# Two weight sums and three low halves of a quad by accumulating loads on GpSimd's queue

## The chip, the cores and the metric

One core of a Trainium2 chip runs the whole program. The metric is the device time of one execution in microseconds (us). Profiles and traces are of one execution each; their times are counted from the start of its span.

## The reference, cut to what matters

One layer of an encoder trunk, for 512 tokens of width 1024 in float32: a gated feed-forward block, a mixer (attention in a neighbourhood beside a pooled branch), a second feed-forward block, and a gated embedding, each normalized before and after and added to the residual. The change lies in the two feed-forward blocks:

```python
D_MODEL = 1024
SEQ = 512
D_FF = 2816

def swiglu(x, w_gate, w_up, w_down):
    return (jax.nn.silu(x @ w_gate) * (x @ w_up)) @ w_down

f = swiglu(rms_norm(h, ffn1_pre_g[i]), ffn1_w_gate[i], ffn1_w_up[i], ffn1_w_down[i])
h = h + 0.5 * rms_norm(f, ffn1_post_g[i])
```

## The kernel before

TensorE multiplies in a rounded float32 form, so every operand is split into a high half `hi` (the value rounded) and a low half `lo` (the value minus `hi`), and a product is three matmuls, at L277 to L279: `hi` with `hi`, `hi` with the other's `lo`, `lo` with the other's `hi`. The weights come as a stream of 195 chunks of 128x1024 float32 (512 KB) from `in_wst`. The class `Stream` loads a chunk on SyncE's queue into a tile `raw` (L207; five buffers), lets ScalarE cast it to `hi` (L243) and VectorE subtract `hi` from it to make `lo` (L244, shown by its helper's line, L165). `hi` and `lo` lie in a tile `w`, of which there are six, so a chunk is split when the product six before it has been multiplied.

The hidden width of a feed-forward block is worked in 11 groups, in three parts of 3, 4 and 4 groups (`PARTS`); each part ends with a down projection over its groups. Groups 3 to 10 (`FAST`), four in each of the last two parts and 16 in the two blocks together, are quads: four weight blocks, a21, a22, a11 and a12, enter seven products of half the width instead of eight (`fast_group`). The operands on the weights' side are

- product 0: a11; 1: a12; 2: a11 + a21 + a22; 3: a21 + a11; 4: a21 + a22; 5: a22; 6: a12 + a11 + a21 + a22.

Products 0, 2, 4 and 6 are summed in PSUM bank `p`, product 1 in `q`, products 3 and 5 in `r`. ScalarE copies `p` to `m1` after product 0, `p` to `acc` after product 2 and `r` to `m7` after product 3 (L477); VectorE adds and subtracts the others. A bank can't be written by the next product before it has been read.

The weight sums are made in `source`: when product 2 is prepared, VectorE makes `both` = a21 + a22 in a buffer of its own (`wsum`), then a21 + a11 in a21's tile and a11 + `both` in a11's tile; for product 6 it adds that to a12. `pump` splits the next chunks in time, at most `NB` = 6 ahead of what has been multiplied; `load` starts loads in the order of the stream, and a chunk's load waits until a tile `raw` is free. The order on each engine is set by the order in which the code is recorded and by a scheduler, which lets an instruction pass others of its engine that it does not depend on. GpSimd has only constants to set at the start.

Of the kernel before, what the change touches and what calls it, by code (L numbers as in the profile page):

```python
# [10 lines left out]
F32 = mybir.dt.float32  # L11
F32R = mybir.dt.float32r
AF = mybir.ActivationFunctionType
ALU = mybir.AluOpType

P = 128
# [7 lines left out]
CH = 1024  # L24
# [2 lines left out]
PARTS = ((0, 3), (3, 7), (7, 11))  # L27
FAST = range(3, 11)
NB = 6
NRAW = 5  # L30
RAW_AHEAD = 2
SPLIT_AHEAD = 4

# [85 lines left out]
def kernel(  # L119
# [9 lines left out]
    nc = tc.nc  # L129
    n_chunks = wst.shape[0]  # L130

    const = ctx.enter_context(tc.tile_pool(name="const", bufs=1))
    wraw = ctx.enter_context(tc.tile_pool(name="wraw", bufs=NRAW))
    wsum = ctx.enter_context(tc.tile_pool(name="wsum", bufs=1))
    wsp = ctx.enter_context(tc.tile_pool(name="wsp", bufs=NB))
    act = ctx.enter_context(tc.tile_pool(name="act", bufs=1))
    tmp = ctx.enter_context(tc.tile_pool(name="tmp", bufs=2))
# [23 lines left out]
    def f32(ap):  # L161
        return ap.bitcast(F32)

    def tt(o, a, b, op):
        nc.vector.tensor_tensor(o, a, b, op=op)  # L165
# [5 lines left out]
    class Stream:  # L171

        LOADS = (3, 4, 4, 4, 4, 4, 4)

        def __init__(self):
            self.ops = []
            self.needs = []
            self.shift = []  # L180
            chunk = 0
            for kind in plan():
                quad = kind == 2
                for i in range(7 if quad else 1):
                    self.ops.append((quad, chunk, i))
                    self.needs.append(chunk + (self.LOADS[i] if quad else 1))
                    self.shift.append(24 if quad and i in (2, 5) else 16 if kind else 0)
                chunk += 4 if quad else 1
            self.n = len(self.ops)
            assert chunk == n_chunks  # L190
            self.loaded = 0
            self.split = 0
            self.done = 0
            self.hold = False
            self.freed = set()
            self.over = set()
            self.raw = {}
            self.parts = {}
            self.both = None

        def load(self, upto):
            while self.loaded < min(upto, n_chunks) and (self.loaded < NRAW or self.loaded - NRAW in self.over):
                c = self.loaded
                self.raw[c] = wraw.tile([P, CH], F32, tag="raw", name=f"raw{c}")
                w = CH // 4 if c < 1 else CH
                for i in range(0, CH, w):
                    nc.sync.dma_start(self.raw[c][:, i:i + w], wst[c][:, i:i + w])  # L207
                self.loaded += 1

        def drop(self, *chunks):  # L210
            for c in chunks:
                del self.raw[c]
                self.over.add(c)

        def source(self, n):

            kind, c, i = self.ops[n]
            if not kind:
                return self.raw[c], (c,)
            a21, a22, a11, a12 = (self.raw.get(c + j) for j in range(4))  # L220
            if i == 2:
                self.both = wsum.tile([P, CH], F32, tag="sum", name="both")
                tt(self.both, a21, a22, ALU.add)
                tt(a21, a21, a11, ALU.add)
                tt(a11, a11, self.both, ALU.add)
            if i == 6:
                tt(a12, a12, a11, ALU.add)
            return ((a11, ()), (a12, ()), (a11, ()), (a21, (c,)), (self.both, ()), (a22, (c + 1,)),
                    (a12, (c + 2, c + 3)))[i]

        def pump(self, upto):
            while self.split < min(upto, self.done + NB, self.n):
                c = self.split
                self.load(self.needs[c])
                assert self.loaded >= self.needs[c]
                raw, over = self.source(c)
                both = wsp.tile([P, 2 * CH + 128], F32R, tag="w", name=f"w{c}")
                b = self.shift[c]
                hi, lo = both[:, b:b + CH], both[:, b + CH + 64:b + 2 * CH + 64]
                w = CH // 4 if c < 1 else CH  # L240
                for i in range(0, CH, w):
                    sl = slice(i, i + w)
                    nc.scalar.copy(hi[:, sl], raw[:, sl])  # L243
                    tt(lo[:, sl], raw[:, sl], f32(hi[:, sl]), ALU.subtract)  # L244
                self.drop(*over)
                self.parts[c] = (hi, lo)
                self.split += 1
                self.load(self.needs[c] + RAW_AHEAD)
# [801 lines left out]
def plan():  # L1050

    def ffn(first):
        out = []
        for g0, g1 in PARTS:
            for g in range(g0, g1):
                out += [2] if g in FAST else [first if g == 0 else 0] * 4
            out += [0] * (g1 - g0) + [int(g1 == PARTS[-1][1])] * (g1 - g0)
        return out

    mixer = [1] * 4 + [0] * (3 * 4 + 1 + 16 + 8 + 4) + [1] * 4  # L1060
    return ffn(0) + mixer + ffn(1) + [0] * 3 + [1] * 8
# [114 lines left out]
```

## Time and profile before

| What | us |
|---|---|
| median of 3 runs | 1083.73 (1081.83 to 1085.82) |
| the profiled execution | 1084.12 |
| its span | 1082.3 |
| TensorE busy | 1060.2 (98%) |
| VectorE busy | 762.3 (70%) |
| ScalarE busy | 544.2 (50%) |
| GpSimd busy | 0.7 |
| SyncE's queue: 107.01 MB | 31.7% of the 16 DMA engines' span |

The profile names engines PE (matmuls), PEld (weight loads), DVE (VectorE), ACT (ScalarE), POOL (GpSimd) and SP (SyncE). A matmul's length is modelled and overlaps the next one's; what counts is the distance of their starts, and the waits. "Idle before" is the time that an engine stood still ahead of a group, with what ended it. The DMA share is the busy share of the 16 DMA engines, which can come out a little over 1 where packets overlap.

### The profile page before, as it was taken

The numbers are of one execution on the slowest core, as the hardware profiler recorded it, in microseconds if no ns is written. First come the engines' busy times: TensorE is split into PE (matmuls) and PEld (weight loads), VectorE is DVE, ScalarE is ACT, GpSimd is POOL, SyncE is SP. The second block draws the span as 40 slices with busy tenths as digits, with TensorE's granted clock in tenths as the row PEclk, the third lists the DMA queues.
The fourth block names the chain that finished last, engine by engine and source line by source line (L and its number), as shares of the span: only waits on it lengthen the run. The fifth ranks groups of instructions, "written<-read, shape, count | busy, mean of one in ns | idle before, by whom it ended". The sixth has DMA issues, their size and how long they took to land.

```text
span 1082.3 us, 16827 instructions
## 1 busy us (share of the span) xinstructions
PE 1060.2 (98%) x6762; PEld 955.9 (88%) x6762; DVE 762.3 (70%) x1279; ACT 544.2 (50%) x921; POOL 0.7 (0%) x6
## 2 busy tenths in 40 slices
PE   9999999999999999999999999999999999999994
PEld 7788999889999988877888899888999889999894
DVE  7893787558854987977444429994787558854976
ACT  8552555235543765366222247752555235543874
POOL 0000000000000000000000000000000000000000
PEclk9999999999999999999999999999999999999997
DMA  8331335223362342231333321342235223341202
GB/s 297 107 104 59 87 109 157 78 78 104 111 178 50 108 153 79 78 98 45 99 96 95 97 76 40 107 133 72 81 115 155 79 79 100 109 162 60 63 17 79
DMA packets 37023, 108.12 MB, mean 100 GB/s; under 512 B 4816, under 2 KB 11472, under 8 KB 36944
## 3 DMA queue, kind: packets, MB, share of 16 engines
q1 hardware_dynamic: 36800, 107.01, 31.7%
q8 instruction: 53, 0.87, 0.3%
q14 instruction: 26, 0.21, 0.1%
q10 hardware_dynamic: 144, 0.03, 0.0%
HBM read 104.93 MB, written 2.10 MB: 99 GB/s over the span
## 4 chain that ended last, share of the span: by engine, by line
PE 90%; DVE 6%; ACT 3%; issue 0%; DMA 0%; DVEq 0%; ACTq 0%
PE g L277 14%; PE g L278 14%; PE g L279 14%; PE p L278 6%; PE p L279 6%; PE p L277 6%; PE r L278 3%; PE r L279 3%; PE r L277 3%; PE gate L279 2%; PE gate L277 2%; PE gate L278 2%; PE q L278 1%; PE q L279 1%; PE q L277 1%; PE br L277 1%
## 5 line engine op out<-in xcount | busy, mean ns | idle before, releaser
L165 DVE TENSOR_TENSOR w<-raw,w 128x1024 fp32r<-128x1024 f32 (+1 forms) x227 | 273.7, 1208 | 152.6 <-ACT w L243 152.4
L243 ACT CAST w<-raw 128x1024 fp32r<-128x1024 f32 (+1 forms) x227 | 234.7, 1038 | 262.1 <-PE g L279 131.5
L277 PE MATMUL g<-zh,w 128*128 128x512 f32 (+1 forms) x512 | 178.6, 349 | 0.0
L278 PE MATMUL g<-zl,w 128*128 128x512 f32 (+1 forms) x512 | 178.3, 348 | 0.0
L279 PE MATMUL g<-zh,w 128*128 128x512 f32 (+1 forms) x512 | 178.3, 348 | 0.0
L279 PE MATMUL g<-uh,w 128*128 128x256 f32 (+1 forms) x448 | 146.5, 330 | 1.4 <-DVE w L165 1.4
L278 PE MATMUL g<-ul,w 128*128 128x256 f32 (+1 forms) x448 | 147.4, 330 | 0.2 <-DVE ul L168 0.2
L277 PE MATMUL g<-uh,w 128*128 128x256 f32 (+1 forms) x448 | 146.4, 331 | 0.6 <-ACT w L243 0.6
L278 PEld LDWEIGHTS g<-zl,w 128*128 128x128 f32 x512 | 96.6, 189 | 12.4
L279 PEld LDWEIGHTS g<-zh,w 128*128 128x128 f32 x512 | 96.2, 188 | 12.6
L277 PEld LDWEIGHTS g<-zh,w 128*128 128x128 f32 x512 | 96.2, 188 | 12.4
L279 PEld LDWEIGHTS g<-uh,w 128*128 128x128 f32 x448 | 84.7, 190 | 9.7 <-DVE w L165 1.6
L278 PEld LDWEIGHTS g<-ul,w 128*128 128x128 f32 x448 | 85.4, 191 | 8.5 <-DVE ul L168 0.6
L277 PEld LDWEIGHTS g<-uh,w 128*128 128x128 f32 x448 | 84.8, 190 | 8.8 <-ACT w L243 0.9
L279 PE MATMUL p<-uh,w 128*128 128x256 f32 x256 | 71.9, 281 | 0.0
L278 PE MATMUL p<-ul,w 128*128 128x256 f32 x256 | 71.9, 281 | 0.0
L277 PE MATMUL p<-uh,w 128*128 128x256 f32 x256 | 71.9, 281 | 0.0
L278 PE MATMUL p<-x,w 128*128 128x256 f32 x256 | 71.5, 279 | 0.0
L278 PE MATMUL r<-x,w 128*128 128x256 f32 x256 | 71.5, 279 | 0.0
L279 PE MATMUL p<-x,w 128*128 128x256 f32 x256 | 71.5, 279 | 0.0
L279 PE MATMUL r<-x,w 128*128 128x256 f32 x256 | 71.4, 279 | 0.0
L277 PE MATMUL p<-x,w 128*128 128x256 f32 x256 | 71.4, 279 | 0.0
(195 smaller groups left out, 2187.6 us busy)
## 6 DMA issues: line engine op xcount, KB each, us to landing
raw<-in_wst SPq DMA_DIRECT2D x191, 512.0 KB, 3.6
h<-in_x SPq DMA_DIRECT2D x8, 256.0 KB, 5.5
bm<-in_bias SPq DMA_DIRECT2D x64, 32.0 KB, 2.2
out<-o SPq DMA_DIRECT2D x16, 128.0 KB, 1.7
raw<-in_wst SPq DMA_DIRECT2D x4, 128.0 KB, 4.0
g_sb<-in_gains ACTq DMA_DIRECT2D x1, 34.0 KB, 3.2
edge_sb<-in_edge SPq DMA_DIRECT2D x1, 32.0 KB, 5.3
```

The costliest lines, as they stand in the source:

```text
L165: nc.vector.tensor_tensor(o, a, b, op=op)
L243: nc.scalar.copy(hi[:, sl], raw[:, sl])
L277: nc.tensor.matmul(o, wh, xh, start=first, stop=False, **kw)
L278: nc.tensor.matmul(o, wh, xl, start=False, stop=False, **kw)
L279: nc.tensor.matmul(o, wl, xh, start=False, stop=last, **kw)
```

## The change

Two sums of a quad are no longer made by VectorE. A quad's loads are now five items instead of four chunks: s3 = a21 + a11, s1 = a21 + a22, a22, a11, a12. For s3 and s1 a plain load on SyncE's queue brings the first block, and a second DMA, issued by GpSimd with `accum_op=add`, adds the second block onto it in SBUF. VectorE still makes a11 + s1 and a12 + a11. The low halves of products 0, 1 and 5, whose operand is a single block, are no longer made by VectorE either: ScalarE writes the negated high half into `lo`, and an accumulating DMA of GpSimd adds the block to it, read from `in_wst` once more. The buffer of `both` goes, and there are six `raw` buffers instead of five; all other tiles keep their places.

```diff
-NRAW = 5
+NRAW = 6
...
-    wsum = ctx.enter_context(tc.tile_pool(name="wsum", bufs=1))
...
-        LOADS = (3, 4, 4, 4, 4, 4, 4)
+        ITEMS = ((0, 2), (0, 1), (1,), (2,), (3,))
+        LOADS = (4, 5, 5, 5, 5, 5, 5)
...
+                n = self.loaded
+                c, *more = self.items[n]
+                self.raw[n] = wraw.tile([P, CH], F32, tag="raw", name=f"raw{n}")
                 w = CH // 4 if c < 1 else CH
                 for i in range(0, CH, w):
-                    nc.sync.dma_start(self.raw[c][:, i:i + w], wst[c][:, i:i + w])
+                    nc.sync.dma_start(self.raw[n][:, i:i + w], wst[c][:, i:i + w])
+                for c in more:
+                    nc.gpsimd.dma_start(self.raw[n], wst[c], accum_op=ALU.add)
                 self.loaded += 1
...
+        def single(self, n):
+
+            quad, c, i = self.ops[n]
+            return self.items[c + {0: 3, 1: 4, 5: 2}[i]][0] if quad and i in (0, 1, 5) else None
...
-            a21, a22, a11, a12 = (self.raw.get(c + j) for j in range(4))
+            s3, s1, a22, a11, a12 = (self.raw.get(c + j) for j in range(5))
             if i == 2:
-                self.both = wsum.tile([P, CH], F32, tag="sum", name="both")
-                tt(self.both, a21, a22, ALU.add)
-                tt(a21, a21, a11, ALU.add)
-                tt(a11, a11, self.both, ALU.add)
+                tt(a11, a11, s1, ALU.add)
             if i == 6:
                 tt(a12, a12, a11, ALU.add)
...
                     nc.scalar.copy(hi[:, sl], raw[:, sl])
-                    tt(lo[:, sl], raw[:, sl], f32(hi[:, sl]), ALU.subtract)
+                    if self.single(c) is None:
+                        tt(lo[:, sl], raw[:, sl], f32(hi[:, sl]), ALU.subtract)
+                    else:
+                        nc.scalar.activation(lo, hi, AF.Copy, scale=-1.0)
+                        nc.gpsimd.dma_start(lo, wst[self.single(c)], accum_op=ALU.add)
```

Three places show how the instructions stand. In them `w25` to `w31` are the seven operands of the second quad of the first block (products 0 to 6), `w32` to `w38` those of the third. Of the items after the change, `raw23` to `raw27` are s3, s1, a22, a11 and a12 of the second quad, `raw28` to `raw32` those of the third, and `raw33` and `raw34` are s3 and s1 of the fourth.

On ScalarE, from product 5 of the second quad to product 2 of the third, before (`raw23` is there a22, `raw25` a12 with its sum, `raw28` a11 and `raw29` a12 of the third quad):

```order
L243 CAST w30_1232<-raw23_931 128x1024
L557 CAST zh_1172<-v_1002 128x512
L477 COPY m1_1206<-p_1176 128x512
L243 CAST w31_1265<-raw25_1063 128x1024
L243 CAST w32_1295<-raw28_1293 128x1024
L584 ACTIVATE w_1235<-w_1235 128x256
L477 COPY acc_107<-p_1176 128x512
L243 CAST w33_1328<-raw29_1298 128x1024
L477 COPY m7_1302<-r_1178 128x512
L243 CAST w34_1364<-raw28_1293 128x1024
```

The same place on ScalarE now:

```order
L251 CAST w30_1238<-raw25_1061 128x1024
L569 CAST zh_1178<-v_1005 128x512
L255 ACTIVATE w30_1238<-w30_1238 128x1024
L489 COPY m1_1212<-p_1182 128x512
L251 CAST w31_1272<-raw27_1069 128x1024
L251 CAST w32_1304<-raw31_1302 128x1024
L596 ACTIVATE w_1242<-w_1242 128x256
L255 ACTIVATE w32_1304<-w32_1304 128x1024
L489 COPY acc_104<-p_1182 128x512
L251 CAST w33_1339<-raw32_1308 128x1024
L255 ACTIVATE w33_1339<-w33_1339 128x1024
L489 COPY m7_1313<-r_1184 128x512
```

A negation (L255) stands now ahead of each of the three copies that free a bank.

On VectorE, from the subtraction for product 5 of the second quad to that for product 3 of the third, before:

```order
L165 TENSOR_TENSOR w30_1232<-raw23_931,w30_1232 128x1024
L165 TENSOR_TENSOR zl_1173<-v_1002,zh_1172 128x512
L165 TENSOR_TENSOR raw26_1065<-raw26_1065,raw28_1293 128x1024
L165 TENSOR_TENSOR w31_1265<-raw25_1063,w31_1265 128x1024
L165 TENSOR_TENSOR w_1235<-q_1177,m1_1206 128x512
L165 TENSOR_TENSOR w32_1295<-raw28_1293,w32_1295 128x1024
L165 TENSOR_TENSOR v_1237<-w_1235 128x256
L165 TENSOR_TENSOR raw28_1293<-raw28_1293,both_1360 128x1024
L165 TENSOR_TENSOR w33_1328<-raw29_1298,w33_1328 128x1024
L165 TENSOR_TENSOR raw29_1298<-raw29_1298,raw28_1293 128x1024
L165 TENSOR_TENSOR w34_1364<-raw28_1293,w34_1364 128x1024
L165 TENSOR_TENSOR w_1331<-m7_1302,p_1176 128x512
```

The same place on VectorE now:

```order
L164 TENSOR_TENSOR zl_1179<-v_1005,zh_1178 128x512
L164 TENSOR_TENSOR w31_1272<-raw27_1069,w31_1272 128x1024
L164 TENSOR_TENSOR w_1242<-q_1183,m1_1212 128x512
L164 TENSOR_TENSOR raw31_1302<-raw31_1302,raw29_1172 128x1024
L164 TENSOR_TENSOR v_1244<-w_1242 128x256
L164 TENSOR_TENSOR raw32_1308<-raw32_1308,raw31_1302 128x1024
L164 TENSOR_TENSOR w34_1373<-raw31_1302,w34_1373 128x1024
L164 TENSOR_TENSOR w_1343<-m7_1313,p_1182 128x512
```

The subtractions for `w30`, `w32` and `w33` and the sum of a21 and a11 are gone; the sum with s1 (`raw29`) and the sum for a12 follow each other.

On GpSimd, which had no DMA before, the accumulating loads from product 5 of the first quad to product 5 of the third stand in this order now:

```order
L256 DMA w23_999<-in_wst 128x1024
L256 DMA w25_1065<-in_wst 128x1024
L213 DMA raw28_1071<-in_wst 128x1024
L256 DMA w26_1100<-in_wst 128x1024
L213 DMA raw29_1172<-in_wst 128x1024
L256 DMA w30_1238<-in_wst 128x1024
L256 DMA w32_1304<-in_wst 128x1024
L213 DMA raw33_1310<-in_wst 128x1024
L256 DMA w33_1339<-in_wst 128x1024
L213 DMA raw34_1411<-in_wst 128x1024
L256 DMA w37_1477<-in_wst 128x1024
```

The low half of a quad's product 1 (`w33`) stands behind the first sum of the next quad (`raw33`), whose plain load must land first. `raw31` takes the buffer that `raw24` leaves, and `raw33` that of `raw27`.

## Rows read from the trace of the kernel before

**Rows 1.** The page's first part: busy us, share of the span, instructions.

```profile
PE 1060.2 (98%) x6762; PEld 955.9 (88%) x6762; DVE 762.3 (70%) x1279; ACT 544.2 (50%) x921; POOL 0.7 (0%) x6
```

**Rows 2.** TensorE's waits in the whole span: total us, times, longest us.

```profile
PE nb L343 <- ACT dh L339: 4.1, 2, 2.2
PE nsum L328 <- DVE acc L165: 4.1, 4, 2.5
PE g L279 <- DVE w L165: 1.4, 1, 1.4
...
PE g L278 <- DVE ul L168: 0.2, 1, 0.2
```

**Rows 3.** Timeline of TensorE: start us, us; starts of products in neighbouring quads.

```profile
129.98 0.28 PE L277 MATMUL p<-uh,w 128*128 128x256 f32 x1
...
135.63 0.28 PE L277 MATMUL p<-x,w 128*128 128x256 f32 x1
...
149.60 0.28 PE L277 MATMUL p<-uh,w 128*128 128x256 f32 x1
...
152.43 0.28 PE L277 MATMUL q<-uh,w 128*128 128x256 f32 x1
```

**Rows 4.** Windows: stretch, us, busy by engine, clock, DMA share, GB/s.

```profile
9.00:18.00 9.00, 9.00 (x40) 7.46 (x39) 8.35 (x12) 8.56 (x14) 0.00 (x0) 1.00 1.03 411
15.00:30.00 15.00, 15.00 (x72) 12.52 (x71) 12.73 (x18) 11.08 (x16) 0.00 (x0) 1.00 0.86 298
...
33.70:36.60 2.90, 2.90 (x8) 2.27 (x8) 2.29 (x4) 0.38 (x1) 0.00 (x0) 0.50 0.46 175
...
120.00:140.00 20.00, 20.00 (x173) 20.00 (x173) 17.58 (x21) 11.58 (x17) 0.00 (x0) 1.00 0.36 106
...
192.00:236.00 44.00, 44.00 (x210) 37.03 (x210) 22.40 (x24) 8.97 (x10) 0.00 (x0) 1.00 0.20 60
```

**Rows 5.** VectorE by line and shape: count | busy us, mean ns | idle before.

```profile
L165 DVE TENSOR_TENSOR w<-raw,w 128x1024 fp32r<-128x1024 f32 x223 | 272.1, 1222 | 152.0 <-ACT w L243 151.8
L165 DVE TENSOR_TENSOR raw<-raw,raw 128x1024 f32<-128x1024 f32 x32 | 39.1, 1222 | 4.6 <-DMA raw<-in_wst 4.0
...
L165 DVE TENSOR_TENSOR both<-raw,raw 128x1024 f32<-128x1024 f32 x16 | 19.5, 1221 | 1.8 <-DMA raw<-in_wst 1.6
```

**Rows 6.** Timeline of TensorE where it waited, in brackets, near 30 and 1022 us.

```profile
32.22 0.39 PE L343 MATMUL nb<-dh,ones_r 128*128 128x256 f32 x1 [1.93 <-ACT dh L339]
...
1023.32 0.50 PE L279 MATMUL g<-uh,w 128*128 128x256 f32 x2 [1.45 <-DVE w L165]
```

**Rows 7.** ScalarE by line and shape: count | busy us, mean ns | idle before.

```profile
L243 ACT CAST w<-raw 128x1024 fp32r<-128x1024 f32 x223 | 233.2, 1049 | 261.6 <-PE g L279 131.5 <-PE gate L279 46.5 <-PE br L279 28.9
...
L312 ACT ACTIVATE uh<-h,g_sb 128x256 fp32r<-128x256 f32 x48 | 23.6, 507 | 8.0 <-DVE h L168 7.9
```

**Rows 8.** Timeline of ScalarE in the second quad.

```profile
132.15 0.62 ACT L557 CAST zh<-v 128x512 fp32r<-128x512 f32 x1 [0.23 <-DVE v L165]
133.00 0.59 ACT L477 COPY m<-p 128x512 f32<-128x512 f32 x1 [0.23 <-PE p L279]
...
135.83 1.05 ACT L243 CAST w<-raw 128x1024 fp32r<-128x1024 f32 x1 [1.29 <-PE q L279]
...
139.06 1.05 ACT L243 CAST w<-raw 128x1024 fp32r<-128x1024 f32 x1
```

**Rows 9.** Timeline of VectorE: subtractions for product 6, and for product 4 later.

```profile
134.90 1.22 DVE L165 TENSOR_TENSOR w<-raw,w 128x1024 fp32r<-128x1024 f32 x1
...
148.11 1.23 DVE L165 TENSOR_TENSOR w<-both,w 128x1024 fp32r<-128x1024 f32 x1 [0.44 <-ACT w L243]
```

**Rows 10.** Line 207, SyncE's loads: issue ns and landing us, min/median/max.

```profile
L207 SPq DMA_DIRECT2D raw<-in_wst x195: 327/328/528, 1.2 to 1026.6; - x195
...
DMA to landing us min/median/max: 2.9/3.6/7.5
```

More of the change, by code (lines that the diff above doesn't have):

```diff
@@ L179, in __init__ @@
             self.needs = []
+            self.items = []
             self.shift = []
@@ L184, in __init__ @@
                 for i in range(7 if quad else 1):
-                    self.ops.append((quad, chunk, i))
-                    self.needs.append(chunk + (self.LOADS[i] if quad else 1))
+                    self.ops.append((quad, len(self.items), i))
+                    self.needs.append(len(self.items) + (self.LOADS[i] if quad else 1))
                     self.shift.append(24 if quad and i in (2, 5) else 16 if kind else 0)
+                self.items += [[chunk + j for j in item] for item in (self.ITEMS if quad else ((0,),))]
                 chunk += 4 if quad else 1
@@ L198, in __init__, with drop @@
             self.parts = {}
-            self.both = None
         def load(self, upto):
-            while self.loaded < min(upto, n_chunks) and (self.loaded < NRAW or self.loaded - NRAW in self.over):
-                c = self.loaded
-                self.raw[c] = wraw.tile([P, CH], F32, tag="raw", name=f"raw{c}")
+            while (self.loaded < min(upto, len(self.items))
+                   and (self.loaded < NRAW or self.loaded - NRAW in self.over)):
+                n = self.loaded
+                c, *more = self.items[n]
+                self.raw[n] = wraw.tile([P, CH], F32, tag="raw", name=f"raw{n}")
                 w = CH // 4 if c < 1 else CH
                 for i in range(0, CH, w):
-                    nc.sync.dma_start(self.raw[c][:, i:i + w], wst[c][:, i:i + w])
+                    nc.sync.dma_start(self.raw[n][:, i:i + w], wst[c][:, i:i + w])
+                for c in more:
+                    nc.gpsimd.dma_start(self.raw[n], wst[c], accum_op=ALU.add)
                 self.loaded += 1
[L210 to L213, printed above, removed]
+        def single(self, n):
+            quad, c, i = self.ops[n]
+            return self.items[c + {0: 3, 1: 4, 5: 2}[i]][0] if quad and i in (0, 1, 5) else None
+        def drop(self, *items):
+            for n in items:
+                del self.raw[n]
+                self.over.add(n)
         def source(self, n):
@@ L219, in source @@
                 return self.raw[c], (c,)
-            a21, a22, a11, a12 = (self.raw.get(c + j) for j in range(4))
+            s3, s1, a22, a11, a12 = (self.raw.get(c + j) for j in range(5))
             if i == 2:
-                self.both = wsum.tile([P, CH], F32, tag="sum", name="both")
-                tt(self.both, a21, a22, ALU.add)
-                tt(a21, a21, a11, ALU.add)
-                tt(a11, a11, self.both, ALU.add)
+                tt(a11, a11, s1, ALU.add)
             if i == 6:
                 tt(a12, a12, a11, ALU.add)
-            return ((a11, ()), (a12, ()), (a11, ()), (a21, (c,)), (self.both, ()), (a22, (c + 1,)),
-                    (a12, (c + 2, c + 3)))[i]
+            return ((a11, ()), (a12, ()), (a11, ()), (s3, (c,)), (s1, (c + 1,)), (a22, (c + 2,)),
+                    (a12, (c + 3, c + 4)))[i]
         def pump(self, upto):
```

## Prediction

> **What bounds the kernel now.** I read the busy times first. TensorE is busy for 98% of the span, VectorE for 70%, ScalarE for 50%, GpSimd for nothing [rows 1]. A busy TensorE alone proves little, so the second view is its waits: nine kinds, from 4.1 down to 0.2 us in total, and none of them stands before a matmul that writes `p`, `q` or `r`, which are the banks of the quads [rows 2]. The third view is the quad itself: the first product of two neighbouring quads starts at 129.98 and 149.60, so one quad takes 19.62 us and one of its seven products 2.80 us [rows 3]. With no wait inside, that is TensorE's own pace. VectorE is fuller there than on average (17.58 of 20 us [rows 4]), but whatever it does is done in time.
>
> So the stage that is changed, 16 quads of 19.62 us (314 us), has nothing to give back: work taken from VectorE there is taken from beside the path. The question is whether what replaces it still hides.
>
> **What leaves.** Per quad VectorE loses two sums (`both`, and the one `raw<-raw,raw` that made a21+a11) and the three subtractions that make the low halves of products 0, 1 and 5: five instructions of 1.22 us [rows 5], 6.1 us a quad, 98 us in all. Worth on the path: 0. The only TensorE wait that names these instructions is one of 1.4 us before 1023.32, where no quad is [rows 2, 6].
>
> **What ScalarE gets.** A negation of 128x1024 for each of the three low halves. Bounds: a scaled activation of 128x256 takes 0.51 us, the cast of 128x1024 1.05 us [rows 7]; I take 1.05, the same shape: 3.1 us a quad, 50 us in all, on an engine busy for 11.58 of 20 us there [rows 4]. Where it stands matters: for product 5 it now lies between the cast of `zh` and the copy of `m1`, which frees bank `p`. That copy began at 133.00; behind a cast of `zh` that ends at 132.77 the negation moves it to 133.8, its end to 134.4, and product 2 needs the bank at 135.63 [rows 3, 8]. Cover left 1.2 us, so nothing, unless the cast ahead of it is late.
>
> **What SyncE gets.** One more 512 KB load a quad (five for four), 16 in all, 0.33 us of issue each on a queue that mostly waits: nothing by itself. But the buffers change: no sum buffer, a sixth raw buffer, and a block's load now follows the release of another one. Block a11 of the third quad (`raw31`) takes over the buffer of `raw24`, the sum of product 4, which VectorE last reads when it makes that product's low half. Such a read ends at 149.34 [rows 9]; a quad earlier that is 129.7. With the median landing of 3.6 us [rows 10] the block is there at 133.3, and its cast starts at 135.83 [rows 8]: 2.5 us of cover. With the longest landing of the trace, 7.5 us, it would be 1.4 us late, and the copies that empty TensorE's banks queue behind that cast on ScalarE.
>
> **What GpSimd's queue gets.** Five accumulating loads of 512 KB a quad, 80 in all, in order: two onto raw tiles, three onto low halves. It has no DMA now, so neither the issue nor the transfer has a row.
> - *Issue.* Nearest row: SyncE's, 0.33 us median, 0.53 at most [rows 10]. Lower bound 0.33; upper bound a whole landing, 7.5 us. Five issues of even 3 us fit into 19.62 us, so I take it as hidden.
> - *Latency of one low half.* Tightest is product 1 of a quad. Its cast runs from 139.06 to 140.11 [rows 8], the negation ends near 141.2, product 1 starts at 152.43 [rows 3]: 11.2 us. An issue of 0.33 us, a landing of 3.6 us and a second stream of 1.3 us make 5.2 us. Ahead of it on the queue stands the sum of the fourth quad, `raw33`; its plain load waits for the buffer that VectorE leaves at 136.12 [rows 9], lands near 139.7, and its accumulation adds at most another 3.6 us of transfer ahead of ours. About 9 of 11.2 us: hidden on engines that are otherwise free.
> - *Transfer.* An accumulation reads the old destination as well as the source for one result. Lower bound: it costs what a plain load of these bytes costs. Upper bound: two plain loads at the slowest rate seen. Nothing excludes either, and below a plain load it can't go, since it moves all of its bytes.
>
> **The DMA engines' sum.** One plain load: in the densest stretch, 9 to 18 us, 411 GB/s at a share of 1.03, 524,288 bytes are 1.28 us of all 16 engines; between 15 and 30 us, 298 GB/s at 0.86 make 347 GB/s when full, 1.51 us; in the quads, 106 GB/s at 0.36, 1.78 us [rows 4]. The engines would be nearly full, so I take the middle of the two dense rows, 1.40 us. A quad goes from four loads (share 0.36) to five plain and five accumulating ones.
> - Accumulation = one plain load: 10 x 1.28 to 1.78 = 12.8 to 17.8 us of 19.62. Hidden.
> - Accumulation = two: 15 x 1.28 to 1.78 = 19.2 to 26.7 us. At 1.40: 21.0 us, 1.4 us more than the quad lasts.
>
> I take two, since two streams in and one out is what the instruction asks for. The first quad of each part of four has its loads and low halves prepared under the down projections before it, where the DMA share is 0.20 [rows 4]; the other 12 pay: 12 x 1.4 = 16.8 us. Where it would appear: TensorE at L279 waiting for a low half, and ScalarE's casts waiting for a load.
>
> The Trainium skill has two rules on this. "Collectives: The Full Stack" (The bandwidth ceiling) says that a reducing DMA reaches half a copy's rate since it reads two sources through one read ring; by it the sum is the second one. No run here shows it yet. "DMA: Bandwidth & Descriptors" (Issuing engines are not separate DMA queues) says that another issuing engine adds no transfer capacity; by it the second queue relieves nothing, and the two queues' loads stand in one sum, as above.
>
> **Forecast.** The profiled execution took 1084.12 us (span 1082.3); the three runs' median is 1083.73, so it is a typical one and is used as it stands. 1084.1 - 0 + 16.8 = 1101 us.
>
> **Rivals.**
> 1. *The transfers stay hidden* (not slower). The mechanism: an accumulation holds a DMA engine little longer than a plain load, because the second read comes from SBUF. The point from which it decides: (19.62 - 5 x 1.40)/5 = 2.52 us of engine time for one accumulation, 1.8 plain loads. Below that the quads run at 19.62 us as now. For: the slack of each low half, and a DMA share of 0.36 now. Against: at two loads it needs the densest rate of the whole trace all the time. Time: 1084 us, 1081 to 1088.
> 2. *Accumulations are dearer than two loads*, by a cost of each row in them. At three loads of 1.40 us a quad asks 20 x 1.40 = 28.0 us, +8.4 us on 12 quads, +101 us: 1185 us. For it and against it the trace has nothing. Long stalls could also cost clock: a wait of 1.93 us was followed by 2.90 us at a granted clock of 0.50, the lower of the two levels, which gives away half of them, 1.45 us; one of 1.45 us by none [rows 4, 6]. At 8 us a quad, if in one piece, that adds up to 12 x 1.45 = 17 us.
> 3. *Capacity suffices, the queue's order doesn't.* A load of a11 that lands late holds ScalarE and with it bank `p`; or GpSimd's issues take over 3 us, and product 1's low half comes late. At 0.5 to 1 us a quad over 16 quads: +8 to +16 us, 1092 to 1100 us. For: 2.5 us of cover against a landing that varies from 2.9 to 7.5 us.
> 4. *Faster.* All of TensorE's waits on VectorE outside the quads come to some 6 us, 4.1 of them before `nsum` [rows 2], most at norms that the change does not touch. Over 5.4 us, 1078 us or less, would need nearly all of them.
>
> **How the numbers follow.** The forecast, two streams over capacity: 0.42, with a range of its own from 1088 (a rate near the dense 1.28 us) to 1169 (1.78 us). Rival 1: 0.40. Rival 2: 0.08. Rival 3: 0.05. Rival 4: 0.05. Forecast and first rival are nearly even, because one unknown decides, and its likely value (two loads) stands next to the point from which it decides (1.8). The range takes in rival 1 whole, rival 3, and the forecast up to its upper end: 1081 to 1170. A measurement of this kernel tells about 0.5% (5.4 us) from no change: slower by more 0.42 + 0.08 + 0.05 = 0.55, within it 0.40, faster 0.05.
>
> **What would show it.** Right: DMA share near 0.9 or more in the quads (0.36 now), a quad longer than 19.62 us, TensorE waits at L279 before `p`, `q` or `r` that end with an accumulating load. Hidden: quads still of 19.62 us with VectorE near 11.5 of 20 us. Rival 3: waits on TensorE at a DMA share below 0.8. The forecast is wrong if an accumulation's packets take about as long as a plain load's, or several times as long.

## The result, and the profile after

The changed kernel took 1113.38 us (median of 4 runs, 1111.16 to 1118.47), the one before 1084.78 beside it (1081.83 to 1085.94): a ratio of 1.0284, 95% interval 1.0268 to 1.0301. It is slower by some 29 us; the forecast was 1101. The profiled execution took 1112.71 us, its span was 1110.9.

The page of the kernel after, its first part, the two large DMA queues of its third part (packets, MB, share of 16 engines), the HBM traffic and the chain that ended last:

```profile
PE 1070.1 (96%) x6762; PEld 964.3 (87%) x6762; DVE 671.8 (60%) x1199; ACT 589.8 (53%) x969; POOL 70.7 (6%) x86
...
q1 hardware_dynamic: 39104, 115.40, 31.4%
q0 software_dynamic: 11520, 41.95, 21.5%
...
HBM read 155.26 MB, written 2.10 MB: 142 GB/s over the span
...
PE 81%; DMA 9%; DVE 4%; ACT 3%; issue 1%; POOL 0%; POOLq 0%; DVEq 0%; ACTq 0%
```

Against [rows 1], VectorE gave up 90.5 us and ScalarE got 45.6 more, as the diff says. Neither moved the end, as runs below show. `q0` is GpSimd's queue: 80 accumulating loads, which were not there before.

TensorE's waits after (total us, times, longest us); [rows 2] had none before `p`, `q` or `r`:

```profile
PE q L291 <- DMA w<-in_wst: 16.9, 6, 5.8
PE nb L355 <- ACT dh L351: 4.1, 2, 2.2
PE nsum L340 <- DVE acc L164: 4.1, 3, 2.5
PE r L291 <- DMA w<-in_wst: 1.9, 4, 0.8
```

The two lines on `w<-in_wst` are new: L291 is the third matmul of a product, the one that needs the low half. The other two stood at the same totals before. `q` is product 1, `r` product 5. So 18.8 of the 29 us are waits for a low half that had not landed.

Where they lie is read from the timeline of TensorE, with the starts of product 1 in the second, third and fourth quad of the first block's last part (part 2 in the table below; columns as in [rows 3]):

```profile
258.49 0.28 PE L289 MATMUL q<-uh,w 128*128 128x256 f32 x1
...
278.75 0.28 PE L289 MATMUL q<-uh,w 128*128 128x256 f32 x1
278.87 0.28 PE L290 MATMUL q<-ul,w 128*128 128x256 f32 x1
282.96 0.56 PE L291 MATMUL q<-uh,w 128*128 128x256 f32 x1 [3.81 <-DMA w<-in_wst]
283.31 0.42 PE L289 MATMUL q<-uh,w 128*128 128x256 f32 x1
283.52 0.41 PE L290 MATMUL q<-ul,w 128*128 128x256 f32 x1
...
287.19 0.28 PE L289 MATMUL p<-x,w 128*128 128x256 f32 x1
...
303.99 0.28 PE L289 MATMUL q<-uh,w 128*128 128x256 f32 x1
```

The second quad lasts 20.26 us from `q` to `q`, the third 25.23; before, each of them lasted 19.62 [rows 3]. Over the four parts with quads (two in each block) the three steps from quad to quad, each of which covers the quad that it starts in, are

| part | first to second | second to third | third to fourth |
|---|---|---|---|
| 1 | 19.62 | 20.35 | 22.27 |
| 2 | 19.62 | 20.26 | 25.23 |
| 3 | 19.62 | 20.89 | 26.12 |
| 4 | 19.62 | 20.35 | 28.45 |

That is 26.8 us over 12 x 19.63, nearly the whole loss, and 23.6 of it lie in the last column, the third quads. The fourth quads lose nothing: from their `q` to that of the next part in the block it is 63.18 us in both kernels. The waits make 18.8 of the 26.8 us; most of the other 8.0 are TensorE's clock. Windows of the kernel after (columns as in [rows 4]): the second quad of a part to the end of the fourth, a wait, what followed it, the stretch behind that, and what followed the longest wait (5.83 us, at 949.40):

```profile
133.07:195.00 61.93, 58.91 (x493) 57.87 (x492) 36.22 (x46) 39.34 (x55) 10.48 (x12) 1.00 0.91 236
...
278.75:284.00 5.25, 1.44 (x9) 1.24 (x8) 1.53 (x2) 1.96 (x3) 0.86 (x1) 0.91 1.06 276
...
283.00:286.20 3.20, 3.20 (x15) 3.20 (x16) 0.00 (x0) 0.00 (x0) 0.00 (x0) 0.50 1.05 273
...
287.20:303.90 16.70, 16.70 (x146) 16.70 (x145) 10.53 (x14) 11.86 (x17) 1.76 (x2) 1.00 0.83 216
...
949.40:955.20 5.80, 5.80 (x27) 5.80 (x28) 0.69 (x1) 0.70 (x1) 0.00 (x0) 0.50 0.87 242
```

Behind the wait of 3.81 us TensorE works for more than 3.2 us at a granted clock of 0.50, the lower of its two levels, and matmuls start 0.21 us apart instead of 0.12 (283.31 and 283.52 against 278.75 and 278.87). Behind 5.83 us it does so for 5.8, and behind the third long wait, 4.79 us before 819.09, for another 3.2. Of these 12.2 us it gives away some 5, an estimate from the two distances; the last 3 of the 8.0 us were not taken apart. The DMA share, 0.36 before, is now 0.83 to 1.06.

Why was this low half late? The timelines of GpSimd (its DMA issues) and of ScalarE there:

```profile
264.24 0.86 POOL L256 DMA_DIRECT2D w<-in_wst  x1 [3.93 <-ACT w L255]
270.98 0.89 POOL L213 DMA_DIRECT2D raw<-in_wst  x1 [5.87 <-DMA raw<-in_wst]
271.61 1.16 POOL L256 DMA_DIRECT2D w<-in_wst  x1
```

```profile
266.48 1.05 ACT L251 CAST w<-raw 128x1024 fp32r<-128x1024 f32 x1 [1.63 <-DMA raw<-in_wst]
267.57 1.06 ACT L255 ACTIVATE w<-w 128x1024 fp32r<-128x1024 f32 x1
```

The negation for product 1 is done at 268.63. The accumulation onto it is issued at 271.61, 3.0 us later, since the next quad's first sum (L213) stands ahead of it on the queue and waits until 270.98 for its plain load. Then it takes 11.3 us to land, at 282.91, and TensorE goes on at 282.96. The times from issue to landing after (us: minimum, median, maximum), of the low halves, of the sums and of SyncE's loads:

```profile
DMA to landing us min/median/max: 5.4/7.7/12.7
...
DMA to landing us min/median/max: 5.4/7.2/13.7
...
DMA to landing us min/median/max: 2.8/4.3/11.9
```

For all 12 low halves of product 1 in second, third and fourth quads, read from the trace in the same way:

| kernel after | issue behind the negation | landing | against the start of product 1 |
|---|---|---|---|
| 6 held up by a sum that waits | 1.0 to 5.4 us | 9.9 to 12.7 us | late, 0.6 to 6.2 us |
| 2 behind a sum that was already issued | 0.4 us | 8.6 and 9.9 us | early by 2.2 and 1.0 us |
| 4 with no sum ahead (fourth quads) | 0.4 us | 5.6 to 9.4 us | early by 2.3 us or more |

### The profile page after: what moved, and what is told of

Same layout as the page of the kernel before. It is cut to its first block, busy times and chain, and to the rows that moved or that the text cites. A ratio compares the mean times of both kernels' runs of the same rounds, so it can differ in the third digit from the quotient of the medians.

```text
span 1110.9 us, 17026 instructions
## 1 busy us (share of the span) xinstructions
PE 1070.1 (96%) x6762; PEld 964.3 (87%) x6762; DVE 671.8 (60%) x1199; ACT 589.8 (53%) x969; POOL 70.7 (6%) x86
## 3 DMA queue, kind: packets, MB, share of 16 engines
q0 software_dynamic: 11520, 41.95, 21.5%
## 4 chain that ended last, share of the span: by engine, by line
PE 81%; DMA 9%; DVE 4%; ACT 3%; issue 1%; POOL 0%; POOLq 0%; DVEq 0%; ACTq 0%
PE g L289 15%; PE g L291 15%; PE g L290 15%; DMA w<-in_wst 5%; DMA raw<-in_wst 4%; PE p L290 3%; PE p L289 3%; PE p L291 3%; PE gate L291 2%; PE gate L290 2%; PE gate L289 2%; PE r L291 2%; PE r L290 2%; PE r L289 2%; ACT w L251 1%; PE br L290 1%
## 5 line engine op out<-in xcount | busy, mean ns | idle before, releaser
L251 ACT CAST w<-raw 128x1024 fp32r<-128x1024 f32 (+1 forms) x243 | 251.4, 1038 | 311.9 <-PE g L291 139.4
L164 DVE TENSOR_TENSOR w<-raw,w 128x1024 fp32r<-128x1024 f32 (+1 forms) x195 | 234.9, 1207 | 195.5 <-ACT w L251 195.1
L291 PE MATMUL g<-zh,w 128*128 128x512 f32 (+1 forms) x512 | 178.4, 348 | 0.0
L291 PE MATMUL g<-uh,w 128*128 128x256 f32 (+1 forms) x448 | 147.6, 332 | 1.4 <-DVE w L164 1.4
L289 PEld LDWEIGHTS g<-zh,w 128*128 128x128 f32 x512 | 96.2, 188 | 12.5
L291 PEld LDWEIGHTS g<-zh,w 128*128 128x128 f32 x512 | 96.3, 188 | 12.4
L291 PEld LDWEIGHTS g<-uh,w 128*128 128x128 f32 x448 | 85.8, 192 | 9.5 <-DVE w L164 1.6
L164 DVE TENSOR_TENSOR raw<-raw,raw 128x1024 f32<-128x1024 f32 x32 | 39.2, 1225 | 57.4 <-ACT w L251 38.9
L291 PE MATMUL r<-x,w 128*128 128x256 f32 x256 | 71.9, 281 | 1.9 <-DMA w<-in_wst 1.9
L213 POOL DMA_DIRECT2D raw<-in_wst x32 | 28.0, 874 | 703.7 <-ACT x L545 423.2
L291 PE MATMUL p<-uh,w 128*128 128x256 f32 x256 | 71.9, 281 | 0.0
L290 PE MATMUL p<-x,w 128*128 128x256 f32 x256 | 71.8, 280 | 0.0
L289 PE MATMUL p<-x,w 128*128 128x256 f32 x256 | 71.7, 280 | 0.0
```

The lines of the kernel that those rows point to most:

```text
L213: nc.gpsimd.dma_start(self.raw[n], wst[c], accum_op=ALU.add)
L289: nc.tensor.matmul(o, wh, xh, start=first, stop=False, **kw)
L290: nc.tensor.matmul(o, wh, xl, start=False, stop=False, **kw)
L291: nc.tensor.matmul(o, wl, xh, start=False, stop=last, **kw)
```

## The experiments

Two theories stood against each other: capacity (an accumulation costs two plain loads, and 15 loads' worth a quad, five plain and five double ones, don't fit) and queue order (product 1's low half stands behind a sum that waits). Unless said otherwise a diff is against the changed kernel; ratios are against the kernel before, run beside them, with 95% intervals.

**The same transfers, plain.**

```diff
-                    nc.gpsimd.dma_start(self.raw[n], wst[c], accum_op=ALU.add)
+                    nc.gpsimd.dma_start(self.raw[n], wst[c])
...
-                        nc.gpsimd.dma_start(lo, wst[self.single(c)], accum_op=ALU.add)
+                        nc.gpsimd.dma_start(lo, wst[self.single(c)])
```

> All five DMAs of a quad on GpSimd's queue stay where they are, but none accumulates: each overwrites its tile with the same 512 KB, so bytes from HBM, issues and queue order are those of the changed kernel and only the second stream (reading the old destination) is gone; sums and low halves are left out of the computation. Theory C (capacity: an accumulation holds the 16 DMA engines for two plain loads, 328 against 159 ns for a 4 KB packet, and 15 loads' worth a quad does not fit into 19.62 us): 10 loads' worth, 14 us at 1.40 us, fits, 1084 to 1088 us. Theory O (queue order: the low half of product 1 is issued some 3 us late, behind the next quad's first sum, which waits for its plain load): the order is unchanged, so part of the loss stays, 1092 to 1105 us.

1083.95 us, ratio 1.0004 (0.9994 to 1.0014). Its two queues, as above:

```profile
q1 hardware_dynamic: 39104, 115.40, 33.1%
q0 software_dynamic: 11520, 41.95, 12.5%
```

The same packets and bytes on `q0` take 12.5% of 1084.1 us (136 us) when they overwrite, 21.5% of 1110.9 us (239 us) when they accumulate: 1.76 times. The median packet of 4 KB on `q0` takes 174 ns here and 328 ns in the changed kernel, 1.89 times; SyncE's plain packets take 159 ns in both, which makes it 2.06 times. So an accumulation does cost about two loads. Issue, waits for buffers, queue order and the ScalarE work are all still in this kernel, and none of them costs time by itself. Queue order alone, for which 1092 us or more was expected, is refuted.

**The order mended.** The two sums of the next quad are recorded behind product 1's low half; all transfers stay.

```diff
-                for c in more:
-                    nc.gpsimd.dma_start(self.raw[n], wst[c], accum_op=ALU.add)
+                self.pending += [(self.raw[n], c, self.split) for c in more]
...
+        def flush(self):
+            while self.pending and self.pending[0][2] <= self.split - LATER:
+                tile_, c, _ = self.pending.pop(0)
...
+                    with tc.issue_after(self.low.ins):
+                        nc.gpsimd.dma_start(tile_, wst[c], accum_op=ALU.add)
```

> The changed kernel with one difference: on GpSimd's queue the next quad's two sums stand behind the low half of product 1 instead of around it, so no low half waits behind a sum's plain load. All transfers are the same. Theory C: the traffic is unchanged, 15 loads' worth a quad; the low half goes out 3 us earlier but the engines are as full, and most of the 28.6 us stays: 1100 to 1113 us. Theory O: the waits of product 1 vanish, 1084 to 1090 us.

1087.2 us, ratio 1.0031 (1.0019 to 1.0042). TensorE's only wait before a product's bank, GpSimd's issues at the place shown above, the window of a part and that of one quad in another part, and the landing of the low halves:

```profile
PE r L303 <- DMA w<-in_wst: 3.2, 3, 1.2
...
264.32 0.89 POOL L267 DMA_DIRECT2D w<-in_wst  x1 [2.19 <-ACT w L266]
267.60 0.87 POOL L225 DMA_DIRECT2D raw<-in_wst  x1 [2.39 <-DVE w L165]
...
132.05:192.00 59.95, 58.89 (x493) 58.27 (x492) 35.87 (x46) 39.52 (x55) 9.62 (x11) 1.00 0.94 239
255.51:275.14 19.63, 19.63 (x170) 19.63 (x169) 11.97 (x16) 13.92 (x20) 4.28 (x5) 1.00 1.02 248
...
DMA to landing us min/median/max: 5.3/7.5/11.0
```

The low half (L267) now goes at 264.32, 0.4 us behind its negation, and the sum (L225) after it. The DMA share is no lower than in the changed kernel (0.94 against 0.91), and yet the 12 steps from quad to quad come to 19.98 us on average instead of 21.87. So capacity alone, for which 1100 us or more was expected, doesn't make the loss either: the traffic nearly fits.

Less than 15 loads' worth moves in one of these steps. In the quad from 255.51 to 275.14, 248 GB/s make 9.3 transfers of 512 KB, and GpSimd issues 5 accumulations in it: 14.3 loads' worth, at a share of 1.02 and without a wait, so 19.63/14.3 = 1.37 us for one at most. Counted from the packets in the trace, with accumulations double, the 12 steps hold 12.1 to 14.6 loads' worth, 13.6 on average (11.6 to 16.0 in the changed kernel, the same 13.6 on average). Of a part's traffic some goes out ahead of the first step, and the fourth quad has no sums of a next one.

**One low half back on VectorE, in two ways.** Once it is product 1's, which takes that one off the queue; once product 5's, which leaves product 1's where it was. Both have 13 loads' worth a quad.

```diff
-            return self.items[c + {0: 3, 1: 4, 5: 2}[i]][0] if quad and i in (0, 1, 5) else None
+            return self.items[c + {0: 3, 1: 4, 5: 2}[i]][0] if quad and i in (0, 5) else None
```

```diff
-            return self.items[c + {0: 3, 1: 4, 5: 2}[i]][0] if quad and i in (0, 1, 5) else None
+            return self.items[c + {0: 3, 1: 4, 5: 2}[i]][0] if quad and i in (0, 1) else None
```

> The low half of product 1 is made by VectorE again; the sums and the low halves of products 0 and 5 stay on GpSimd's queue. Theory C: 5 plain loads and 4 accumulations are 13 loads' worth, 16.6 us at 1.28 and 18.2 at 1.40 of 19.62 us: fits barely, 1084 to 1092 us. Theory O: the one transfer that was late is gone, 1084 us.

> The low half of product 5 is made by VectorE again; the sums and the low halves of products 0 and 1 stay on GpSimd's queue, product 1's still behind the next quad's first sum. Theory C: the same 13 loads' worth as without product 1's, so the same time within 5 us, 1084 to 1092 us. Theory O: product 5's transfer was never the late one and the order is unchanged, 1100 to 1113 us.

1084.82 us, ratio 1.0010 (0.9997 to 1.0022), and 1085.1 us, ratio 1.0017 (1.0002 to 1.0031). What is left of the waits before a product, in the first and in the second:

```profile
PE r L291 <- DMA w<-in_wst: 1.6, 1, 1.6
```

```profile
PE q L291 <- DMA w<-in_wst: 1.4, 1, 1.4
...
131.21:190.00 58.79, 58.79 (x494) 58.31 (x493) 39.20 (x49) 37.41 (x52) 7.59 (x9) 1.00 0.84 214
```

The second one decides: the bad order is still there, and with two loads' worth a quad fewer (a share of 0.84 over that part) it costs a single wait, in the last third quad, where the low half was again issued 2.7 us late and landed after 10.4 us. In the other eleven the lag is 1.4 us or less. Queue order alone doesn't make the loss, and neither does capacity alone. It takes both.

**Sums alone, low halves alone.** The diffs are against the changed kernel and against the kernel before.

```diff
-            return self.items[c + {0: 3, 1: 4, 5: 2}[i]][0] if quad and i in (0, 1, 5) else None
+            return None
```

```diff
-                    tt(lo[:, sl], raw[:, sl], f32(hi[:, sl]), ALU.subtract)
...
+                        nc.scalar.activation(lo, hi, AF.Copy, scale=-1.0)
+                        nc.gpsimd.dma_start(lo, wst[self.single(c)], accum_op=ALU.add)
```

> The two sums of a quad stay accumulating loads; the three low halves are VectorE's subtractions again and ScalarE's negations are gone. By loads' worth a quad: 5 plain + 2 accumulations = 9 instead of 15, DMA share about 9/15 of the 0.88 of the changed kernel, near 0.53. Theory I (the loss needs both nearly full engines and product 1's low half behind the next quad's first sum): the low half is off the queue and the engines are half empty, so quads of 19.62 us, no wait before p, q or r, 1083 to 1085 us. Rival (accumulating onto a raw tile is itself late, since plain load and accumulation follow each other before a product's cast): waits before p or r that end with raw, 1088 us or more.

> The kernel before with the three low halves of a quad by negation and accumulating load, the two sums on VectorE as before, five raw buffers: 4 plain + 3 accumulations = 10 loads' worth a quad, DMA share near 0.6, and nothing that waits for a plain load stands ahead of a low half on GpSimd's queue. Theory I: quads of 19.62 us, product 1's low half lands some 6 us after its negation, 1083 to 1085 us. Rival (the negation ahead of the copies that free the banks, or the landing of a low half by itself, costs time): waits before p, q or r, 1088 us or more.

1083.21 us, ratio 0.9996 (0.9984 to 1.0008), and 1083.58 us, ratio 0.9999 (0.9986 to 1.0012). A part in the first; in the second a part and the landing of its low halves:

```profile
129.59:188.50 58.91, 58.91 (x495) 58.42 (x494) 44.07 (x53) 33.49 (x48) 3.34 (x4) 1.00 0.64 175
```

```profile
132.18:191.00 58.82, 58.82 (x495) 58.33 (x494) 39.63 (x49) 39.79 (x56) 6.09 (x7) 1.00 0.79 196
...
DMA to landing us min/median/max: 5.4/5.7/8.1
```

Every quad lasts 19.62 or 19.63 us. Each half of the change is free by itself; the share is above what was expected (0.64 for 0.53, 0.79 for 0.6), so it doesn't grow in proportion to the loads. The negations in front of the copies that free the banks cost nothing.

**No accumulating load at all.** The two places that issue them are taken out of the changed kernel.

> No accumulating load at all: the two sums' second blocks and the blocks of the three low halves are left out of the computation, and so are VectorE's instructions for them; loads, buffers, ScalarE's negations and the order stay. It bounds what the idea could give if its transfers were free. Theory (the quads are at TensorE's own pace, VectorE's 98 us are taken from beside the path): 1083 to 1085 us, quads of 19.62 us. Rival (VectorE's load delays TensorE somewhere that the waits don't show): faster by several us, 1078 or less.

1083.62 us, ratio 0.9997 (0.9988 to 1.0007), with VectorE at the changed kernel's load:

```profile
PE 1059.2 (98%) x6762; PEld 954.7 (88%) x6762; DVE 671.9 (62%) x1199; ACT 589.6 (55%) x969; POOL 0.7 (0%) x6
```

With its transfers free, the change would have brought nothing. VectorE's work was beside the path, and the quads kept 19.62 or 19.63 us.

**More transfers, order mended.** These diffs show what is added to the kernel with the order mended. First four 128 KB loads a quad on SyncE's queue, into one small tile:

```diff
+                if n in self.extra:
+                    idle = scr.tile([P, CH // 4], F32, tag="idle", name="idle")
+                    nc.sync.dma_start(idle, wst[c][:, 0:CH // 4])
```

> The kernel with the order mended (product 1's low half ahead of the next quad's two sums, all 15 loads' worth a quad) and, added on SyncE's queue, four loads of 128 KB a quad into a tile that nobody reads: 16 loads' worth. It looks for the edge of the capacity. By the forecast's 1.40 us a load the kernel without the extra would already be over it, and with it a quad would last 16 x 1.40 = 22.4 us: +2.8 us on 12 quads, 34 us, about 1120 us. By the share seen in quads of the changed kernel (0.88 of 19.62 us for 15 loads' worth, 1.15 us each) 16 make 18.4 us: still inside, quads of 19.6 us with longer landings, 1087 to 1095 us by single waits for late low halves.

1123.47 us, ratio 1.0364 (1.0339 to 1.0389), near the 1120 of the forecast's unit, and yet no proof of it. SyncE's queue waits, TensorE's longest kind of wait, and a window of its quads:

```profile
SPq L221 <- DMA idle<-in_wst: 166.3, 61, 6.9
...
PE p L308 <- ACT acc L508: 29.9, 3, 14.0
...
132.00:152.00 20.00, 15.91 (x137) 15.71 (x135) 7.71 (x11) 6.52 (x10) 2.63 (x3) 1.00 0.76 180
```

Each of the four loads waits for the one before it, since they share a tile, and all of the kernel's loads stand behind it on the queue: 166 us of waits at a DMA share of only 0.76. This run measured the queue and not the capacity. Its 64 loads also didn't keep to their quads: all were issued between 32.0 and 249.7 us. The first part's steps last 27.08 to 35.35 us, the other nine 19.62 to 21.25. In part 2 from 271.34 to 330.22 us, with no extra load left, three steps pass without a wait and hold 43.3 loads' worth by their packets: 58.88/43.3 = 1.36 us for one at most. In its place the extra transfers went to memory outside the core, where no instruction waits for them, meant for once and twice a quad:

```diff
+    idle = nc.dram_tensor("idle", (32, P, CH), F32, kind="Internal").ap()
...
+                if n in self.extra:
+                    nc.sync.dma_start(idle[self.spare], wst[c])
+                    self.spare += 1
```

> The order mended, and one more 512 KB plain transfer a quad on SyncE's queue, from in_wst into memory outside the core that nobody reads, so that no instruction waits for it: 16 loads' worth. In place of the earlier run with four 128 KB loads, in which SyncE's queue waited for each of them and the DMA share stayed near 0.8. Capacity by the dense row (1.28 us a load): 15 make 19.2 us and fit, 16 make 20.5 us, +0.86 us on 12 quads, 10 us: about 1097 us, DMA share near 1. By the forecast's 1.40 us: 22.4 us a quad, +33 us, 1120 us. By 1.15 us (a share of 0.88 for 15): 18.4 us, still 1087 us.

> As the run before, with two such transfers a quad: 17 loads' worth. By 1.28 us: 21.8 us a quad, +2.1 us on 12 quads, 26 us: about 1113 us. By 1.40 us: 23.8 us, +50 us, 1137 us. By 1.15 us: 19.6 us, at the edge, 1087 to 1092 us.

1098.66 us, ratio 1.0132 (1.0104 to 1.0159), and 1142.06 us, ratio 1.0529 (1.0502 to 1.0556). A part of the first with its share:

```profile
131.92:198.00 66.08, 61.06 (x493) 60.05 (x492) 35.65 (x46) 39.11 (x56) 9.60 (x11) 0.95 0.92 251
```

The first total is within 2 us of what 1.28 us a load gave, the second near the 1137 of 1.40 us, but neither run measures 16 or 17 loads' worth a quad. What nothing waits for, nothing holds back: in the trace the 16 extra transfers of the first run are issued between 31.9 and 406.1 us, one in each of the six steps of the first block and none in those of the second, whose quads begin after 750 us. The six steps with an extra come to 21.87 us on average, the six without to 20.30. In the second run all 32 are issued between 32.0 and 686.6 us, and part of its loss is stalls (the share falls to 0.52 between 172 and 192 us, and low halves are late for `q` and `p`). What the runs do show is that little room is left: six more transfers among the quads go with some 11 us more than in the order-mended kernel (1098.66 against 1087.2). Where the edge lies is open, and so is whether a transfer that also writes outside the core counts as one load.

## Why the prediction was right or wrong, point by point

- **Bound and what leaves: right.** TensorE's own pace bounds the quads. VectorE lost 90.5 us for the 98 forecast, worth 0 (the run without accumulations shows it).
- **ScalarE: right.** A negation takes 1057 ns (1.05 forecast), and the low halves alone cost nothing.
- **Issue on GpSimd: right.** 0.87 us at the median, inside the bounds and hidden.
- **An accumulation is two loads: right.** 1.76 times by the queue's share, 1.89 to 2.06 by the packet. That it reads two sources at half a copy's rate is what "Collectives: The Full Stack" (The bandwidth ceiling) of the Trainium skill has for reducing DMAs; these numbers agree with it roughly.
- **The engines' sum: too large, by its amount first.** The forecast let 15 loads' worth move in each of 12 quads; the packets show 13.6 on average in the 12 steps. The unit of 1.40 us was a little high: 1.36 to 1.37 us at most where TensorE didn't wait. 13.6 x 1.37 = 18.6 us fit into 19.62 us on average, where the forecast had 21.0. Capacity was given 16.8 us; the order-mended kernel, with every transfer still in it, loses 3, and its waits before a bank are for product 5's low half.
- **The latency of product 1's low half: wrong, and this is what cost the time.** The slack of 11.2 us (10.1 to 12.1 in the 12 cases of the table) and the sum ahead on the queue were read rightly. The landing was taken from [rows 10] with 3.6 us, from a kernel whose quads run at a share of 0.36, for engines that the next paragraph of the same forecast put near 1. There it took 8.6 to 12.7 us wherever a sum stood ahead, and where the sum waited for its plain load the issue came 1.0 to 5.4 us late on top. The sum was "about 9 of 11.2 us"; in the example it was 3.0 + 11.3 = 14.3 of 10.1 us. The text did say "on engines that are otherwise free", and then did not ask what it would be on full ones.
- **12 quads pay, the first of a part doesn't: right as to the first, wrong as to the fourth.** The first and the fourth lose nothing; the second quads lose 3.3 us in all and the third 23.6.
- **Clock: named under the second rival, left out of the sum.** It took some 5 us by the estimate above. The 2.90 us there are the length of the window that was read, not of the stretch at the lower clock.
- **The rivals.** The first (hidden) fell with the measured 1.0284. The third, queue order, named the place but called it a case in which capacity suffices, and gave 8 to 16 us. It needs the full traffic, and then costs 26 us (1113.4 against 1087.2). The mark given for it, waits at a share below 0.8, was wrong too: they came at 0.91.
- **What would show it.** The share of 0.91, the longer quads and the waits before `q` and `r` all came, but they don't tell the forecast from the third rival at full engines; only the mended order did. ScalarE's casts waiting for a load, named there too, came once, with 1.6 us.
- **The number** came within 12 us of the measured one, with the right sign and in the range. That was luck: two errors went against each other, an overrun of capacity that was too large, and a late low half that was not in the sum.

Not settled: why a landing grows to 10 us and more behind a sum. The trace shows sum and low half in flight together. With product 5's low half back on VectorE, the eight low halves of product 1 behind a sum still land after 8.3 to 10.4 us, and the four in fourth quads, with none ahead, after 5.4 to 6.2; but a fourth quad also has other transfers around it, and no run separated the two.

## What to carry to other kernels

A transfer's landing time belongs to the share at which it was read: before loads are added, take it again at the share that they will make, and hold it against the slack of the tightest consumer. On an in-order DMA queue an issue that has to wait goes behind one that is ready and urgent; here that order alone is worth 26 us at 15 loads' worth a quad and next to nothing at 13. And work that is taken from an engine beside the path pays for no traffic at all.

## What the runs showed of the hardware that was not expected

- The DMA share doesn't grow in proportion to the load. Counted by packets from `q` to `q`, a step with 4.0 loads' worth shows about 0.35 (before), one with 10.0 about 0.80 (low halves alone), one with 14.2 1.02 (order mended): 1.7, 1.6 and 1.4 us of all engines for each. Over a part, 0.91 cost 29 us in one order, and 0.94 cost 3 in the other.
- In the changed kernel an accumulation of 512 KB lands after 5.4 us at best and 12.7 to 13.7 us at worst, where a plain load lands after 2.8 to 11.9.
- The lower clock stays on after the wait is over. Behind waits of 3.81 and 4.79 us TensorE works at 0.50 for 3.2 us and more, behind 5.83 us for 5.8, behind 1.93 us for 2.9 and more [rows 4, 6]; behind the wait of 1.50 us before 155.31 the clock stays at 1.00.
